# Attention scores of two heads in turns in the two row halves of TensorE, and conditioning sums stored chunk by chunk

## The chip, the cores and the metric

The kernel runs on one core of a Trainium2 chip. The metric is the device time of one execution in microseconds. A core has TensorE (PE; its weight loads are listed as PEld), VectorE (DVE), ScalarE (ACT), GpSimd (POOL) and SyncE (SP, which issues nearly all DMA transfers here).

## The reference

One batch of 256 tokens of width 1024 goes through two blocks, all in fp32. Cut to what matters:

```python
# first block
mod = silu(c) @ ada_w + ada_b                 # 6 vectors of 1024
h = rms_norm(x) * (1 + sc1) + sh1
q, kv, gates, u, merge_g = split(h @ w_in)    # 16 heads of 64, 4 key heads
attn = g0 * compressed(q, kv) + g1 * selected(q, kv) + g2 * windowed(q, kv)
x = x + g1 * merge(attn, state_space(u))
x = x + g2 * hier_moe(rms_norm(x) * (1 + sc2) + sh2)     # 32 experts
x = rms_norm(x)
# second block
mod, mod_c = silu(c_2) @ w_mod + b_mod, silu(c_ctx) @ w_mod + b_mod
x = x + gt1 * rmsnorm(neighbourhood_attention(...) , grouped_attention(...))
x = x + gt2 * rmsnorm(moe(...))                          # 32 experts, top 4
```

With 256 tokens every block of 64 keys is selected and the window covers all tokens, so the selected and the windowed branch are both plain causal attention. That is 16 heads x 2 branches = 32 looks of 256 x 256 scores.

## The kernel before, in words

The program is one long list of instructions; in the parts spoken of here PE, ACT, DVE and POOL run exactly in the order in which the program writes them. Weights come through a ring of 2 MB tiles: SP loads the next piece as soon as the oldest one has been released (`used`).

**The stream.** Projections of the first mixer are cut into rows (`block`, `feed`): one credit of `feed(n)` is three PE matmuls (L705, a product of high and low parts), and after certain rows ACT and DVE finish a result. `cut_ahead` splits the next weights (ACT L717, DVE L718).

**The attention of the first mixer.** `Look(n)` is one head of one branch; looks 2k and 2k+1 are a pair whose queries and keys lie in partitions 0 to 63 and 64 to 127. `scores` takes a PSUM tile `sc` (there are two) and multiplies a 64-row slice of the queries with the keys: 128 keys for the first 128 queries (L1282), 256 keys for the others (L1283). Each fp32 matmul is two passes, so a look has four weight loads and four matmuls there. Then `largest` (DVE, L1288 to L1290), `exps` (ACT, L1295, L1296), `scaled` (DVE, L1300 to L1303), `turned` (PE transposes, L1308), `copied` (ACT, L1312), and for a pair `values` (PE, L1326; ACT L1328) and `ended` (DVE, L1333, only for the second branch: every fourth step). The loop over i has 35 steps and is a pipeline: step i does `largest(i)`, `scores(i+1)`, `scaled(i-1)`, `exps(i)`, two credits of the stream, on odd steps the values of pair (i-3, i-2), one turn of the conditioning generator, `turned(i-1)`, and one more credit.

**The conditioning vectors.** A product of a 1024-vector with 1024 x 512 weights is summed on ACT, DVE and POOL into one tile of 128 x 512 partial sums (`sums` L1143, `part` L1958), or by PE into four strips which ACT copies out (`mod_rows`, L460). The sum over the partitions is then made by PE with those partial sums as the stationary operand and a column of ones as the moving one: eight matmuls, two passes each, of 64 columns (`mod_sum` L481, `pick` L469). Vector element 8p+c goes to partition p, so chunk c is every eighth element of the tile.

Of the kernel before, what the change touches and what calls it, by code (L numbers as in the profile page):

```python
# [17 lines left out]
ALU = mybir.AluOpType  # L18
# [3 lines left out]
P = 128  # L22
D = 1024
T = 256
# [133 lines left out]
def _body(tc, nc, a, off, es, stop, dump):  # L158
    V, S, G, PE = nc.vector, nc.scalar, nc.gpsimd, nc.tensor
# [4 lines left out]
    def ps(tag, bufs, name=None):  # L164
        return psum.tile([P, 512], F32, tag=tag, bufs=bufs, name=name or tag)
# [279 lines left out]
    def used(key):  # L445

        released.add(key)
        while ring.used < ring.loaded and ring.pieces[ring.used][0] in released:
            ring.done()

    def mod_rows(key, lhs, into=None):

        w = ring.get(key).rearrange("p (c f) -> p c f", c=8)
        pt = mmps()
        for c in range(8):
            j = c % 4
            PE.matmul(pt[32 * j:32 * j + 32, :], bcast(lhs[:, c, :], [P, 32]), w[:, c, :], start=(c < 4), stop=(c >= 4), tile_position=(0, 32 * j))
        used(key)
        rows = into[:, :512] if into is not None else pp.tile([P, 512], F32, tag="modrows", bufs=2, name="rows")
        S.copy(rows, pt)  # L460
        return rows

    def pick(pt, h, rows, sel=None):

        sel = k("ecol") if sel is None else sel
        n = sel.shape[1]
        rv = rows.rearrange("q (p c) -> q c p", c=8)
        for c in range(8):
            PE.matmul(pt[64 * h:64 * h + 64, n * c:n * c + n], rv[:, c, :], sel, start=True, stop=True, tile_position=(0, 64 * h))  # L469

# [4 lines left out]
    def mod_sum(s, h, dst, bias):  # L475

        r = slice(64 * h, 64 * h + 64)
        pt = trps()
        sv = s.rearrange("q (p c) -> q c p", c=8)
        for c in range(8):  # L480
            PE.matmul(pt[r, c:c + 1], sv[:, c, :], k("ones")[:, 0:1], start=True, stop=True, tile_position=(0, 64 * h))  # L481
        add_bias(dst[r], pt[r], bias[r])
# [182 lines left out]
    pt = trps()  # L665
# [85 lines left out]
    def feed(n):  # L751

        feed.credit += n
        while feed.credit > 0 and (stream or after):
            cost = 1
            if not feed.apart or not cut_up:
                cut_ahead()
            while lows and (len(lows) == len(cut_up) or not feed.apart and lows[0][3] + feed.lag <= feed.done):
                finish_low()
            if stream:  # L760
                _, _, _, products, rows, post = stream[0]
                cost = 4 // rows
                products(feed.row, cut_up[0])
                feed.row += 1
                if feed.row == rows:
                    feed.row = 0
                    stream.popleft(), cut_up.popleft()
                    after.extend([delay, f] for delay, f in post)
            feed.credit -= cost
            for item in after:  # L770
                item[0] -= cost
            for item in [x for x in after if x[0] < 0]:
                after.remove(item)
                item[1]()
            feed.done += cost
            while feed.done > feed.next:
                feed.next += STEP0
                next(feed.behind, None)
        if not stream and not after:
            feed.credit = 0  # L780
# [333 lines left out]
    def vectors_on():  # L1114

        pending = None
        for tag, v, h in vectors:
            key = (tag, v, h)
            while key not in ring.tiles:
                yield  # L1120
            if tag == "wmod":
                if pending:
                    pending()
                    pending = None
                rows = mod_rows(key, cs2, sums)
                yield
                yield
                pt = trps()
                r = slice(64 * h, 64 * h + 64)
                pick(pt, h, rows, k("esel"))  # L1130
                add_bias((sh3, sc3)[v][r], pt[r], bm[r, v])
                yield
                continue
            w = ring.get(key).rearrange("p (c f) -> p c f", c=8)
            for c in range(0, 8, 2):
                S.activation(w[:, c], w[:, c], AF.Identity, scale=cs[:, c])
                if c:
                    G.tensor_tensor(w[:, 0], w[:, 0], w[:, c], op=ALU.add)
                    V.scalar_tensor_tensor(w[:, 1], w[:, c + 1], cs[:, c + 1], w[:, 1], op0=ALU.mult, op1=ALU.add)
                else:  # L1140
                    V.tensor_scalar(w[:, 1], w[:, 1], cs[:, 1], None, op0=ALU.mult)
                if c == 6:
                    G.tensor_tensor(sums, w[:, 0], w[:, 1], op=ALU.add)  # L1143
                    used(key)
                if c == 4 and pending:
                    pending()
                    pending = None
                yield

            def pending(v=v, h=h, key=key):  # L1150
                mod_sum(sums, h, (gc[:, 0], sh2, sc2, gc[:, 1])[v - 2], ab[:, v])
                summed.append(key)
        if pending:
            pending()
# [112 lines left out]
    class Look:  # L1267
# [7 lines left out]
            self.g, self.gp = 2 * gp + s, gp  # L1275
            self.h = 4 * self.g + self.i

        def scores(self):
            self.pt = pt = ps("sc", 2)
            r = slice(64 * self.s, 64 * self.s + 64)  # L1280
            q, kk = qT[r, self.blk], kz[r, self.br, self.gp]
            PE.matmul(pt[:, :P], q[:, :P], kk[:, :P], start=True, stop=True, tile_position=(64 * self.s, 0))  # L1282
            PE.matmul(pt[:, P:P + T], q[:, P:], kk, start=True, stop=True, tile_position=(64 * self.s, 0))  # L1283

        def largest(self):
            self.e = e = pw.tile([P, 512], F32, tag=f"rot{self.n % 3}", name="e")[:, :384]
# [43 lines left out]
    def ended(pair):  # L1330
        if pair[0].br:
            blk = pair[0].blk
            V.tensor_tensor(ap_[1][:, blk, :], Look.po[:, :T], ap_[0][:, blk, :].bitcast(F32), op=ALU.subtract)  # L1333

    looks = [Look(n) for n in range(32)]
    for n in range(2):
        compressed_scores(n)
        feed(LOOK[0])
    looks[0].scores()
    feed.apart = True  # L1340
    for i in range(35):
        st = looks[i] if i < 32 else None
        prev = looks[i - 1] if 0 < i < 33 else None
        pair = looks[i - 3:i - 1] if i % 2 and i > 2 else None
        if st:
            st.largest()
        if i < 31:
            looks[i + 1].scores()
        if prev:
            prev.scaled()  # L1350
        if st:
            st.exps()
        if lows and len(cut_up) - len(lows) < 2:
            finish_low()
        feed(LOOK[1])
        if pair:
            values(pair)
            ended(pair)
        cut_ahead()
        next(feed.behind, None)  # L1360
        if i < 2:
            compressed_weights(i)
        if i == 4:
            compressed_turned(0)
            compressed_turned(1)
        if prev:
            prev.turned()
            prev.copied()
        feed(LOOK[2])
# [565 lines left out]
    def conditions():  # L1935

        ready, fresh = None, 0
        for i in range(9):
            if i < 8:
                key = ("wmod", 2 + i // 2, i % 2)  # L1940
                while key not in ring.tiles:
                    fresh = WAIT2
                    yield
                for _ in range(fresh):
                    yield
                fresh = 0
                w = ring.get(key).rearrange("p (c f) -> p c f", c=8)
                s = pk.tile([P, 512], F32, tag="part", bufs=2, name="part")
            for c in range(0, 8, 2):
                if i < 8:  # L1950
                    S.activation(w[:, c], w[:, c], AF.Identity, scale=cs2[:, c, 0:1])
                    if c:
                        G.tensor_tensor(w[:, 0], w[:, 0], w[:, c], op=ALU.add)
                        V.scalar_tensor_tensor(w[:, 1], w[:, c + 1], cs2[:, c + 1, 0:1], w[:, 1], op0=ALU.mult, op1=ALU.add)
                    else:
                        V.tensor_scalar(w[:, 1], w[:, 1], cs2[:, 1, 0:1], None, op0=ALU.mult)
                    if c == 6:
                        G.tensor_tensor(s, w[:, 0], w[:, 1], op=ALU.add)  # L1958
                        used(key)
                if c == 4 and i:  # L1960
                    v, h = 2 + (i - 1) // 2, (i - 1) % 2
                    mod_sum(ready, h, (gc[:, 2], sh4, sc4, gc[:, 3])[v - 2], bm[:, v])
                    summed.append(i)
                    if i == 8:
                        return
                yield
            ready = s
# [884 lines left out]
```

## Time and profile before

| | |
|---|---|
| median of the runs, lowest to highest | 2046.55 us, 2046.46 to 2049.3 us (3 runs) |
| the profiled execution | 2040.22 us, span of its instructions 2038.5 us |
| busy in the span | PE 1767.2 us (87%), PEld 990.5 (49%), DVE 854.2 (42%), ACT 544.2 (27%), POOL 258.6 (13%) |
| mean granted TensorE clock | 0.931 of full |
| DMA | 630.82 MB, mean 309 GB/s |

Busy time of PE is modelled from pipelined matmuls, so the distance between starts says more than the busy time. The profile also gives the idle time before an instruction and what ended it; "issue" there means that nothing which the profile shows was waited for.

### The profile page before, as it was taken

What the parts mean: (1) busy time and instruction counts of PE and PEld (TensorE: products, weight loads), DVE (VectorE), ACT (ScalarE), POOL (GpSimd) and SP (SyncE); (2) the same over time, 40 slices, a digit from 0 to 9 for tenths busy, and PEclk for the clock granted to TensorE, in tenths of its full rate; (3) what the DMA queues carried; (4) which work ended last, traced back from release to release, by engine and by line L of the source; (5) the groups of instructions that cost most, each with busy time, mean ns of one, the idle gap of its engine ahead of it and who ended that gap; (6) DMA issues with size and microseconds to landing.
All of it is one profiled execution on the core that took longest, in us unless ns stands there. A gap on an engine that the chain in (4) does not pass through costs nothing. (4 is left out here: it accounts for less than half of the span.)

```text
span 2038.5 us, 25531 instructions
## 1 busy us (share of the span) xinstructions
PE 1767.2 (87%) x10043; PEld 990.5 (49%) x10043; DVE 854.2 (42%) x1832; ACT 544.2 (27%) x1184; POOL 258.6 (13%) x232
## 2 busy tenths in 40 slices
PE   5898999998898997899999689886899889999865
PEld 3766777876445536678864123332233333333211
DVE  7998878543312237886644112211121221221112
ACT  4442566332001115565532011110021111121001
POOL 2576312110000003630110000000000000000000
PEclk8898889898999998899979899998899999999986
DMA  8634235867889977743347999999999999899996
GB/s 262 232 114 161 99 124 179 276 239 271 319 319 395 393 294 214 256 172 94 151 167 326 420 420 419 425 422 422 416 422 419 421 423 419 340 420 418 424 421 252
DMA packets 172666, 630.82 MB, mean 309 GB/s; under 512 B 25424, under 2 KB 32016, under 8 KB 152048
## 3 DMA queue, kind: packets, MB, share of 16 engines
q1 hardware_dynamic: 172112, 628.04, 79.3%
q8 instruction: 89, 1.46, 0.3%
q10 hardware_dynamic: 288, 0.52, 0.1%
q0 software_dynamic: 128, 0.39, 0.1%
q14 instruction: 49, 0.40, 0.1%
HBM read 627.88 MB, written 1.05 MB: 309 GB/s over the span
## 5 line engine op out<-in xcount | busy, mean ns | idle before, releaser
L2553 PE MATMUL mm<-w,xT 128*64 128x512 f32 x1472 | 329.3, 601 | 1.3 <-DMA w<-in_w_gu 1.3
L2553 PEld LDWEIGHTS mm<-w,xT 128*64 128x64 f32 x1472 | 102.8, 138 | 204.2 <-issue 197.4
L2644 PE MATMUL o<-w,aT 128*64 128x512 f32 x640 | 150.7, 606 | 2.5 <-DMA w<-in_w_dn 2.5
L2587 PE MATMUL mm<-w,xT 128*32 128x512 f32 x768 | 104.6, 675 | 39.9 <-DMA w<-in_w_gu 39.9
L2562 DVE TENSOR_SCALAR g<-mm 128x512 f32<-128x512 f32 x23 | 15.9, 692 | 262.7 <-PE mm L2553 262.7
L2821 POOL TENSOR_TENSOR fin<-acc,fin 128x512 f32<-128x512 f32 x1 | 1.3, 1275 | 975.6 <-DVE acc L2819 975.6
L718 DVE TENSOR_TENSOR lo<-w,hi 128x512 fp32r<-128x512 f32 x126 | 102.2, 824 | 26.9 <-ACT hi L717 24.9
L705 PE MATMUL mm<-hTh,scratch 128*128 128x256 f32 x392 | 98.3, 317 | 10.0 <-DVE scratch L718 10.0
L717 ACT CAST hi<-w 128x512 fp32r<-128x512 f32 x126 | 76.7, 620 | 62.0 <-PE mm L705 54.2
L2619 PE MATMUL o<-w,aT 128*32 128x512 f32 x384 | 69.1, 752 | 25.7 <-DMA w<-in_w_dn 23.9
L2644 PEld LDWEIGHTS o<-w,aT 128*64 128x64 f32 x640 | 45.1, 139 | 87.5 <-issue 80.3
L2564 ACT ACTIVATE s<-g 128x512 f32<-128x512 f32 x23 | 14.5, 632 | 272.9 <-DVE g L2562 272.9
L705 PEld LDWEIGHTS mm<-hTh,scratch 128*128 128x128 f32 x392 | 71.7, 204 | 28.1 <-issue 14.1
L1657 PE MATMUL mm<-w,xT 128*32 128x512 f32 x640 | 74.4, 612 | 6.6 <-DVEq L1843 2.7
L2659 DVE SCALAR_TENSOR_TENSOR yl<-yy,wc,yh 128x512 fp32r<-128x512 f32 (+1 forms) x30 | 21.4, 748 | 137.4 <-ACT yh L2658 137.2
L2587 PEld LDWEIGHTS mm<-w,xT 128*32 128x32 f32 x768 | 23.0, 117 | 108.1 <-DMA w<-in_w_gu 61.9
L705 PE MATMUL mm<-hT3h,lo 128*128 128x256 f32 x192 | 60.6, 316 | 8.7 <-DVE lo L718 6.1
L2649 ACT COPY yy<-o 64x512 f32<-64x512 f32 x40 | 23.2, 580 | 157.6 <-PE o L2644 157.2
L1632 PEld LDWEIGHTS sc<-Sm,x 128*128 128x128 f32 x256 | 61.6, 334 | 6.6 <-issue 5.0
L2674 DVE TENSOR_TENSOR acc<-acc,sc 128x512 f32<-128x512 f32 x56 | 37.0, 685 | 66.4 <-PE sc L2666 66.4
L1632 PE MATMUL sc<-Sm,x 128*128 128x128 f32 x256 | 63.1, 410 | 1.3 <-DVE Sm L1623 1.2
L705 PE MATMUL mm<-scratch 128*128 128x256 f32 x216 | 63.8, 295 | 0.0
(706 smaller groups left out, 3532.0 us busy)
## 6 DMA issues: line engine op xcount, KB each, us to landing
w<-in_w_gu SPq DMA_DIRECT2D x128, 2048.0 KB, 20.3
w<-in_w_dn SPq DMA_DIRECT2D x63, 2048.0 KB, 23.2
w<-in_w_in SPq DMA_DIRECT2D x20, 2048.0 KB, 9.5
w<-in_moe_w_gate SPq DMA_DIRECT2D x32, 1024.0 KB, 10.5
w<-in_moe_w_up SPq DMA_DIRECT2D x32, 1024.0 KB, 12.5
w<-in_moe_w_down SPq DMA_DIRECT2D x32, 1024.0 KB, 13.8
w<-in_ada_w SPq DMA_DIRECT2D x12, 2048.0 KB, 9.8
w<-in_w_mod SPq DMA_DIRECT2D x12, 2048.0 KB, 8.9
```

The source lines that it names most:

```text
L705: PE.matmul(out, x, y, start=start and i == 0, stop=stop and i == 2)
L717: S.copy(hi, src)
L718: return parts, lambda: V.tensor_tensor(lo, src, hi.bitcast(F32), op=ALU.subtract)
L1632: PE.matmul(pt[:, P * cc:P * cc + P], xv1[:, n, c, :], Sm[:, n].rearrange("p e s -> p (e s)"), start=(n == 0), stop=(n == 1))
L1657: PE.matmul(pg[32 * j:32 * j + 32, :].rearrange("p (j f) -> p j f", j=2), xT[:, c, 32 * j:32 * j + 32], w[:, c % 2], start=(c == 0), stop= ...
L2553: PE.matmul(pg[i][64 * j:64 * j + 64, :], bcast(ident[:, q:q + 1], [P, 64]) if c < 0 else xT[:, c, :], bgu if c < 0 else w[:, o:o + 512], ...
L2587: PE.matmul(pg[32 * t:32 * t + 32, :], xT[:, c, :], w[:, 512 * ij:512 * ij + 512], start=False, stop=(c == 7), tile_position=(0, 32 * t))
L2619: PE.matmul(pd[32 * t:32 * t + 32, :], aT[:, f % 4, 2 * (1 - e) + f // 4, :], w[:, 512 * j:512 * j + 512], start=False, stop=(f == 7), til ...
L2644: PE.matmul(pd[64 * j:64 * j + 64, :], aT[:, f % 4, f // 4, :], w[:, 512 * j:512 * j + 512], start=False, stop=(f == 7), tile_position=(0, ...
L2649: S.copy(y[:, 512 * j:512 * j + 512], pd[64 * j:64 * j + 64, :])
L2659: V.scalar_tensor_tensor(yl[:, o], y[:, o], back[1], yh[:, o].bitcast(F32), op0=ALU.mult, op1=ALU.subtract)
L2674: V.tensor_tensor(o, o, pc, op=ALU.add)
```

## The change

`scores` becomes `score(n)`, one of the two products of a look. `both_scores` issues them for a pair in turns: first product of the head in rows 0 to 63, first product of the head in rows 64 to 127, then the two second products. The first pair is issued ahead of the loop. In the loop `scores(i+1)` is gone from each step; on odd steps `both_scores` of looks i+1 and i+2 stands after the two credits of the stream, ahead of `values`.

The partial sums are stored with chunk c contiguous (64 elements in a row): ACT's copy in `mod_rows` and POOL's last add now write with a step of 64 elements, and the weight loads of `pick` and `mod_sum` read 64 neighbouring elements where they read every eighth.

```diff
+    def by_chunk(t):
+        return t.rearrange("q (c p) -> q p c", c=8)
...
-        S.copy(rows, pt)
+        S.copy(by_chunk(rows), pt.rearrange("q (p c) -> q p c", c=8))
...
-        rv = rows.rearrange("q (p c) -> q c p", c=8)
+        rv = rows.rearrange("q (c p) -> q c p", c=8)
...
-        sv = s.rearrange("q (p c) -> q c p", c=8)
+        sv = s.rearrange("q (c p) -> q c p", c=8)
...
-                    G.tensor_tensor(sums, w[:, 0], w[:, 1], op=ALU.add)
+                    G.tensor_tensor(by_chunk(sums), w[:, 0].rearrange("q (p c) -> q p c", c=8), w[:, 1].rearrange("q (p c) -> q p c", c=8), op=ALU.add)
...
-        def scores(self):
-            self.pt = pt = ps("sc", 2)
+        def score(self, n):
+            if n == 0:
+                self.pt = ps("sc", 2)
             r = slice(64 * self.s, 64 * self.s + 64)
             q, kk = qT[r, self.blk], kz[r, self.br, self.gp]
-            PE.matmul(pt[:, :P], q[:, :P], kk[:, :P], start=True, stop=True, tile_position=(64 * self.s, 0))
-            PE.matmul(pt[:, P:P + T], q[:, P:], kk, start=True, stop=True, tile_position=(64 * self.s, 0))
+            if n:
+                PE.matmul(self.pt[:, P:P + T], q[:, P:], kk, start=True, stop=True, tile_position=(64 * self.s, 0))
+            else:
+                PE.matmul(self.pt[:, :P], q[:, :P], kk[:, :P], start=True, stop=True, tile_position=(64 * self.s, 0))
...
+    def both_scores(pair):
+        for n in range(2):
+            for st in pair:
+                st.score(n)
...
-    looks[0].scores()
+    both_scores(looks[0:2])
...
             st.largest()
-        if i < 31:
-            looks[i + 1].scores()
         if prev:
             prev.scaled()
...
         feed(LOOK[1])
+        if i % 2 and i < 31:
+            both_scores(looks[i + 1:i + 3])
         if pair:
             values(pair)
```

The add into `part` (L1958) changes as the one into `sums` does.

## Rows read from the trace of the kernel before

**Rows 1.** Page, part 2: DMA share of 40 equal slices, in tenths.
```profile
DMA  8634235867889977743347999999999999899996
```

**Rows 2.** Stretches: us, busy (x instructions) PE, PEld, DVE, ACT, POOL; clock; DMA share, GB/s.
```profile
213.00:333.00 120.00, 114.54 (x717) 87.84 (x716) 96.88 (x338) 73.27 (x209) 33.77 (x25) 0.89 0.33 117
370.00:420.00 50.00, 50.00 (x362) 40.51 (x362) 18.44 (x33) 15.10 (x24) 7.37 (x6) 0.88 0.86 269
800.00:920.00 120.00, 106.97 (x706) 87.42 (x706) 101.40 (x217) 69.27 (x161) 53.65 (x49) 0.91 0.65 223
1030.00:2038.00 1008.00, 852.20 (x4154) 311.02 (x4152) 223.58 (x446) 146.96 (x295) 7.08 (x12) 0.93 0.95 393
```

**Rows 3.** Weight loads grouped by line and shape: count, busy us, mean ns; idle before.
```profile
L1632 PEld LDWEIGHTS sc<-Sm,x 128*128 128x128 f32 x256 | 61.6, 334 | 6.6 <-issue 5.0 <-DVE Sm L1623 1.6
...
L481 PEld LDWEIGHTS tr<-C,sums 128*64 128x64 f32 x128 | 16.1, 215 | 0.7
...
L1070 PEld LDWEIGHTS tr<-w,lk 128*64 128x64 f32 x32 | 4.2, 137 | 2.3
```

**Rows 4.** Weight loads in order of time: start us, length us of the whole run.
```profile
207.90 1.87 PEld L1230 LDWEIGHTS sc<-kcz,qT 128*128 128x128 f32 x16
...
217.29 1.99 PEld L481 LDWEIGHTS tr<-C,sums 128*64 128x64 f32 x16
```

**Rows 5.** Matmuls around one look's scores, in order of time.
```profile
261.92 0.28 PE L705 MATMUL mm<-scratch,third 128*128 128x256 f32 x1
262.03 0.28 PE L705 MATMUL mm<-hTh,third 128*128 128x256 f32 x1
262.24 0.49 PE L1282 MATMUL sc<-kz,qT 64*128 64x128 f32 x2
...
263.09 0.39 PE L705 MATMUL mm<-hTh,third 128*128 128x256 f32 x1
```

**Rows 6.** The weight load after those scores, with the idle time before it.
```profile
263.09 0.19 PEld L705 LDWEIGHTS mm<-hTh,third 128*128 128x128 f32 x1 [0.33 <-issue]
```

**Rows 7.** Second mixer: a pair's scores, eight matmuls in the two row halves in turns.
```profile
931.44 0.28 PE L705 MATMUL mm<-hT3h,hi 128*128 128x256 f32 x1
931.65 0.70 PE L2099 MATMUL sc<-kbT,qbT 64*128 64x256 f32 x4
...
932.72 0.39 PE L705 MATMUL mm<-hT3h,lo 128*128 128x256 f32 x1
```

**Rows 8.** Attention loop after a pair of the second branch, in order of time.
```profile
271.05 0.55 PE L1308 MATMUL tr<-C,e 128*128 128x128 f32 x3
...
271.56 0.42 DVE L1333 TENSOR_TENSOR attnT<-o,attnT 128x256 fp32r<-128x256 f32 x1 [2.35 <-ACT attnT L1328]
...
273.24 0.35 DVE L1303 TENSOR_SCALAR e<-e,su 128x256 f32<-128x256 f32 x1
...
273.54 0.55 PE L1308 MATMUL tr<-C,e 128*128 128x128 f32 x3
```

**Rows 9.** Groups of ACT and POOL: count, busy us, mean ns; idle before.
```profile
L460 ACT COPY sums<-mm 128x512 f32<-128x512 f32 x4 | 2.3, 586 | 17.6 <-PE mm L457 17.6
...
L491 ACT COPY g1b<-tr 128x512 f32<-128x512 f32 x2 | 2.2, 1076 | 5.3 <-PE tr L490 5.3
...
L1143 POOL TENSOR_TENSOR sums<-w 128x512 f32<-128x512 f32 x8 | 11.0, 1378 | 1.3 <-DVE w L1139 0.7
...
L1063 POOL TENSOR_TENSOR lk<-kx,posT 128x960 f32<-128x960 f32 x1 | 2.6, 2592 | 0.0
```

**Rows 10.** DVE beside POOL in the loop, in order of time.
```profile
279.61 1.27 POOL L1138 TENSOR_TENSOR w<-w 128x512 f32<-128x512 f32 x1 [26.65 <-ACT w L1136]
279.65 1.26 DVE L1290 TENSOR_SCALAR mx<-mx 128x2 f32<-128x2 f32 x1
```

**Rows 11.** Start of the kernel: the last pick and what waited for it.
```profile
40.88 2.08 PE L469 MATMUL sc<-C,rows 128*64 128x1 f32 x16 [1.82 <-ACT rows L460]
...
43.00 0.17 DVE L473 TENSOR_TENSOR sc<-sc,ab 128x8 f32<-128x8 f32 x1 [0.58 <-PE sc L469]
```

More of the change, by code (lines that the diff above doesn't have):

```diff
@@ L1957, in conditions @@
                     if c == 6:
-                        G.tensor_tensor(s, w[:, 0], w[:, 1], op=ALU.add)
+                        G.tensor_tensor(by_chunk(s), w[:, 0].rearrange("q (p c) -> q p c", c=8), w[:, 1].rearrange("q (p c) -> q p c", c=8), op=ALU.add)
                         used(key)
```

## The prediction

> **What bounds the kernel now.** I read the DMA slices first. The reader is to see that from about the twenty-second slice on (1030 us) DMA is full: the second mixture of experts runs at the pace of its weights [rows 1]. But that stretch can't begin before routing, which comes at the end of everything before it. So time won ahead of 1030 us moves the whole stretch forward, as long as the earlier part isn't limited by DMA itself. The table of stretches comes next: in the attention loop (213 to 333 us) PE is busy 114.5 of 120 us, DVE 96.9, and DMA only a third; from 370 to 420 us PE is busy all the time, with DMA at 0.86; in the second mixer's start (800 to 920 us) PE has 107 and DVE 101 of 120 us [rows 2]. The changed instructions lie in these three stretches and in the first 45 us. In all of them PE leads, in the loop and the second mixer with DVE close behind. That closeness is what the sum has to be cut for.
>
> The sum is made against the profiled execution, 2040.2 us. The median of the runs is 2046.55 us, 0.3% above it; I subtract the gain from the median. A difference below about 0.2%, 4 us, can't be told from none.
>
> **The sums of the conditioning vectors.** One group is 16 weight loads of 64 columns with one or two moving columns each. There are 24 groups: 8 of L481 on `sums` (217 to 378 us), 8 on `part` (810 to 918 us), and 4 + 4 of L469 (24 to 41 and 389 to 417 us). The group in the rows takes 1.99 us for 16 loads: 15 pitches and a last load of 0.215, so 0.118 a load; the next thing on PE starts 2.0 us later, 0.125 a load [rows 3, 4]. What would a contiguous load take? Single loads of 64 columns from neighbouring elements last 137 ns, those of every eighth element 215 [rows 3]. The same step in 128-column loads (L1632) lasts 334 ns, and contiguous ones 0.19 us [rows 3, 6]. The pitch is told by L1230: 16 contiguous loads of 128 columns in 1.87 us, (1.87 - 0.19) / 15 = 0.112 each, so 0.056 for 64 columns if pitch goes with columns [rows 4, 6]. No row has 64 contiguous columns with so few moving ones, so the bounds are 0.056 and, if small matmuls have a floor of their own, the present 0.125. I take 0.056, since the difference of the single durations, 215 - 137 = 78 ns a load, says nearly the same as 0.125 - 0.056 = 69. A group saves 16 x 0.069 = 1.1 us, at most 16 x 0.078 = 1.25.
>
> The Trainium skill speaks against this: "TensorE: Matmul & The Clock Gate", section "LDWEIGHTS (loading the stationary operand)", makes the time of a load a matter of the column count alone, 64 / 1.2 = 53 ns for 64 columns, an estimate by that page. By it storing chunks contiguously would save nothing; the durations of 215 and 137 ns for the same 64 columns go against it.
>
> **Where these savings reach the end.** *Start:* only the last pick is on the path; DVE's next step of the chain waits 0.58 us for it [rows 11]. ACT's copy becomes slower (below), so 0.5 us, between 0 and 1. *Loop:* six groups, 6.6 us if PE leads throughout. Where DVE has the last word a PE saving is lost; DVE fills 97 of 120 us [rows 2], so I take two thirds, 4.5. *345 to 420 us:* two groups and four picks, 6.6 us; PE is busy throughout from 370 on, one of the two groups lies before, and DMA at 0.86 leaves it little room to start its loads earlier [rows 2]. I take 5. *800 to 920 us:* eight groups, 8.8 us, DVE at 101 against PE at 107 [rows 2]: half, 4.5.
>
> **What the new order of storing costs.** ACT's eight copies write with a step of 64 elements. ACT's nearest row is a copy of the same size with a step of eight on the writing side: 1076 against 586 ns [rows 9]. That is 0.5 us for each; behind the copies `pick` follows two turns of the generator later (in the loop's tail), so only the last one at the start shows, counted there. POOL's 16 last adds take 1378 ns. POOL's nearest row with a step is L1063, 2592 ns for 960 elements, 2.7 ns an element, or 1382 for 512 [rows 9]: nothing. That step is on the reading side; if writing costs POOL what it costs ACT, 1076 / 586 = 1.84 times, an add takes 2.5 us. I take nothing, as the row is of the same engine, and keep +1.15 us an add. It could matter because a small DVE operation lasted 1.26 us while a POOL addition of 1.27 us ran [rows 10]: what POOL gains in length, DVE can lose. The next tile's load, which the add releases, would be later by as much; with DMA at a third it is hidden in the loop.
>
> **The scores.** A look costs PE, from the last stream matmul to the next, 263.09 - 262.03 = 1.06 us, where the normal pitch is 0.11: 0.95 us for a look, 1.90 for two. A third of it is the gap of 0.33 us in which PE's loads stand still after the scores [rows 5, 6]. The second mixer already issues a pair in turns: 932.72 - 931.44 = 1.28, less 0.11, 1.17 us for eight matmuls of 256 columns [rows 7]. The new pair has four of 256 and four of 128, so 1.17 is its upper bound; halving two of the four rounds can't take more than 0.3 off. I take 1.1. A pair so saves 0.8 us (0.73 to 1.0), through one gap instead of two and through loads and matmuls of the two halves side by side. 16 pairs: 12.8 us, if PE leads.
>
> It doesn't all the time. Every fourth step DVE waits for the values (2.35 us idle), then does `ended`, `largest` and `scaled`, up to 273.24 + 0.35 = 273.59, and PE's next transposes start at 273.54, just as DVE is done [rows 8]. From the transposes at 271.05 to these PE has had a credit, a look's scores and two credits to do. The change takes the scores (0.95) out of just this stretch and puts them ahead of the values: there PE will arrive 0.8 to 0.9 us early and wait for DVE. That happens once per two pairs, 8 times: 8 x 0.85 = 6.8 us, though the values themselves come 2 x 0.95 - 1.1 = 0.8 us earlier per pair, which is the gain already counted. So 12.8 - 6.8 = 6 us with no help, and up to 12.8 if DVE also finds its inputs sooner. In two pairs PE's own work is 12.1 us before and 10.5 after; DVE's, by its share in the loop, 12.1 x 97 / 120 = 9.8. The cycle can't get shorter than DVE's 9.8, nor does it quite reach 10.5; I take 11.1, 1.0 us a cycle, 8 us in all.
>
> The pair needs both `sc` tiles free: `largest(i)` must be done before the second head's matmuls. It stands first in DVE's step, two credits and one `scaled` ahead, so no wait is counted; queued behind it on PE would be the values, and DVE's `ended` behind these.
>
> **Sum:** 0.5 + 4.5 + 5 + 4.5 + 8 = 22.5 us: 2017.7 for a profiled execution, 2046.55 - 22.5 = 2024 us for the median. Own range 2014 to 2033.
>
> **The rivals.** *All of it counts* (DVE is pulled along): 1 + 6.6 + 6.6 + 8.8 + 12.8 = 36 us, 2010.5 us. For it: PE is busy in every one of these stretches. Against: DVE's share. *Few columns have a floor of their own:* groups stay at 2.0 us whatever the step, only the scores pay: 8 us, 2038.5. For it: no row with 64 contiguous columns and one moving; against: 215 and 137 ns. By the page of the Trainium skill named above, "TensorE: Matmul & The Clock Gate", the groups would stay as long for another reason, with the same time. *DVE takes over at once:* loop and second mixer give nothing but 2 us between them, 0.5 + 5 + 2 = 7.5 us, 2039. For it: the tight hand-over at 273.5 us and the DVE shares; against: DVE still idles 23 us in the loop. *The gain is swallowed by weights that come no earlier:* 2046.5. Against: DMA at a third in the loop. *POOL's strided writes hold DVE* (the other side): 14 of the 16 adds stand beside the loop and the second mixer. Each microsecond that they get longer can cost DVE 14 us there. With 2.5 us an add that is 14 x 1.15 = 16 us, a gain of 6; slower than before by 0.2% it gets when an add passes 1.38 + 26.6 / 14 = 3.3 us, and at 3.6 us the time is 2055. Nothing in the trace shows POOL that slow in such an add.
>
> **How the numbers follow.** Forecast 0.52; all of it 0.14; floor 0.10; DVE at once 0.13; swallowed 0.06; POOL 0.05. The likeliest gives 2024 us. The range goes from 2010 us (all of it) to 2040 us (floor and DVE at once are in), and leaves out the last two and some of the ends of the first ones, under 0.2. Faster by over 0.2% (under 2042.5 us): 0.52 + 0.14 + 0.10 + 0.13 = 0.89; within 0.2%: 0.06; slower: 0.05.
>
> **What would show it.** The groups of L481 and L469: 16 loads in about 1.0 us instead of 2.0, single loads near 137 ns. A pair's four lines of scores: about 1.1 us up to the next work on PE, and the gap of 0.33 us once a pair or not at all. In the loop: PE idle before L1308 after each fourth step, released by DVE L1303, some 0.8 us. The loop ends about 12 us earlier, the second mixture of experts starts some 22 us earlier and takes as long as before. POOL's adds near 1.4 us, ACT's L460 near 1.1. I am wrong if the loads stay at 215 ns, if PE's waits for DVE in the loop exceed 12 us, or if the 1008 us of the last stretch grow.

## The result and the profile after

The change is faster: 2020.68 us (median of 4 runs, 2020.03 to 2024.68) against 2046.51 us (4 runs); the ratio is 0.9877, with a 95% interval from 0.9859 to 0.9894. The forecast was 2024 us. The profiled executions lie 19.35 us apart, 2040.22 and 2020.87 us, since the one profiled before was faster than each of the four runs.

The slices of the page after, DMA share in tenths as in [rows 1], and the same stretches as [rows 2]:

```profile
DMA  8624337976899986742457999999999999899996
```

```profile
213.00:333.00 120.00, 96.46 (x778) 77.33 (x777) 107.37 (x363) 78.21 (x225) 38.58 (x29) 0.94 0.42 132
370.00:420.00 50.00, 44.87 (x353) 36.63 (x353) 23.94 (x42) 20.56 (x33) 13.20 (x13) 1.00 0.87 305
800.00:920.00 120.00, 102.87 (x742) 80.26 (x742) 105.20 (x235) 71.39 (x170) 45.63 (x44) 0.93 0.57 192
1030.00:2019.00 989.00, 841.30 (x4068) 297.17 (x4067) 212.89 (x409) 141.33 (x279) 2.38 (x3) 0.93 0.96 396
```

In the attention loop PE falls from 114.5 to 96.5 us of 120 while DVE rises from 96.9 to 107.4: DVE now has the larger share, in the loop and in the second mixer. Part of DVE's rise is that the same 120 us hold more of the loop (363 DVE instructions against 338). The last stretch is full of DMA as before; it begins 22.0 us earlier (DVE's first `ordr` at 1041.24 us against 1063.28).

The weight loads, against [rows 3] by line and shape (count, busy us, mean ns; idle before), and against [rows 4] in order of time (start, length of the run):

```profile
L1645 PEld LDWEIGHTS sc<-Sm,x 128*128 128x128 f32 x256 | 61.6, 335 | 6.6 <-issue 5.0 <-DVE Sm L1636 1.6
...
L485 PEld LDWEIGHTS tr<-C,sums 128*64 128x64 f32 x128 | 8.9, 146 | 1.0 <-issue 0.3
...
L1074 PEld LDWEIGHTS tr<-w,lk 128*64 128x64 f32 x32 | 4.2, 137 | 2.3
```

```profile
207.43 1.87 PEld L1234 LDWEIGHTS sc<-kcz,qT 128*128 128x128 f32 x16
...
240.56 1.01 PEld L485 LDWEIGHTS tr<-C,sums 128*64 128x64 f32 x16
```

A single load of the sums takes 146 ns where it took 215, and 16 of them 1.01 us where they took 1.99. The loads whose reading was not changed (L1645, L1074, L1234) last what they lasted. The pitch is (1.01 - 0.146) / 15 = 0.058 us; 0.056 was forecast. The Trainium skill ("TensorE: Matmul & The Clock Gate", section "LDWEIGHTS (loading the stationary operand)") makes 64 columns 53 ns, an estimate by that page, by their count alone; the contiguous pitch of 0.058 us nearly agrees, the 0.118 us worked out from [rows 4] for every eighth element does not.

The storing side, against [rows 9] (same columns):

```profile
L464 ACT COPY sums<-mm 128x512 f32<-128x512 f32 x4 | 4.3, 1076 | 11.4 <-PE mm L461 11.4
```

```profile
L1971 POOL TENSOR_TENSOR part<-w 128x512 f32<-128x512 f32 x8 | 11.4, 1419 | 5.1 <-DVE w L1967 4.1 <-DVE su L2140 0.7
L1147 POOL TENSOR_TENSOR sums<-w 128x512 f32<-128x512 f32 x8 | 10.9, 1360 | 2.3 <-DVE w L1143 1.8
```

ACT pays 0.49 us a copy for the step of 64, as its row of another copy had told. POOL pays nothing: 1360 ns against 1378 for `sums`, 1419 against 1409 for `part`.

A pair's scores, against [rows 5], as matmuls in order of time:

```profile
258.61 0.28 PE L709 MATMUL mm<-hTh,third 128*128 128x256 f32 x1
258.82 0.49 PE L1291 MATMUL sc<-kz,qT 64*128 64x128 f32 x4
259.14 0.60 PE L1289 MATMUL sc<-kz,qT 64*128 64x256 f32 x4
259.67 0.87 PE L1334 MATMUL o<-eT,vt 128*64 128x256 f32 x8
```

From the last stream matmul to the next work on PE it is 1.06 us, less the pitch of 0.11: 0.95 us for a pair. That is what one look took before. Why shows in PE's first matmuls of the scores, up to 262.4 us before and up to 258.95 us after:

```profile
262.24 0.37 PE L1282 MATMUL sc<-kz,qT 64*128 64x128 f32 x1
```

```profile
258.82 0.38 PE L1291 MATMUL sc<-kz,qT 64*128 64x128 f32 x2
```

One matmul of a single look lasts 0.37 us, and two of a pair, one of each head, are over within 0.38 us: they start 7 ns apart, and so do the three pairs of matmuls that follow. The two row halves work at the same time.

And the step behind a pair of the second branch, against [rows 8], in order of time on PE and DVE:

```profile
265.49 0.55 PE L1316 MATMUL tr<-C,e 128*128 128x128 f32 x3
...
266.01 0.42 DVE L1341 TENSOR_TENSOR attnT<-o,attnT 128x256 fp32r<-128x256 f32 x1 [1.40 <-ACT attnT L1336]
...
267.49 0.29 DVE L1310 TENSOR_SCALAR e<-e,su 128x128 f32<-128x128 f32 x1
267.69 0.35 DVE L1311 TENSOR_SCALAR e<-e,su 128x256 f32<-128x256 f32 x1
267.92 0.61 PE L1316 MATMUL tr<-C,e 128*128 128x128 f32 x3 [0.82 <-DVE e L1310]
```

PE now stands idle for 0.82 us ahead of these transposes; 0.85 was forecast. In the steps behind the loop's first seven `ended` such a wait lasts 0.81 to 1.60 us, 8.4 us together. Over the whole loop these waits are (waiting line, releaser: us in total, times, longest), before and after:

```profile
PE tr L1308 <- DVE e L1302: 4.2, 6, 1.5
```

```profile
PE tr L1316 <- DVE e L1310: 21.1, 17, 3.4
```

PE is no longer the engine that leads there, so what counts more is what DVE itself waits for. The same for DVE, for the values and for the scores, before and after:

```profile
DVE attnT L1333 <- ACT attnT L1328: 14.6, 7, 4.0
DVE e L1288 <- PE sc L1283: 4.1, 3, 2.2
```

```profile
DVE attnT L1341 <- ACT attnT L1336: 11.4, 7, 3.4
DVE e L1296 <- PE sc L1289: 0.2, 1, 0.2
```

With 1.5 us more for the sums before, that is 20.2 us of waits before and 11.6 after. DVE's work in the loop is 107.5 and 108.3 us. Work and waits together fall short of the loop's length below by 3.7 us both times, and by 3.5 to 3.9 us in all twelve kernels of this study. So the loop lasts as long as DVE works and waits, and a change gains there what it takes off DVE's waits.

Where the time came from is best read between landmarks that every kernel has. The loop runs from ACT's first `pcm` to DVE's last `ended`; the tail from there to DVE's first `lg` of the first routing; the second mixer's sums from ACT's first `zr` to its last `oaTh`; the last stretch from DVE's first `ordr` to its last `acc`.

| us | loop | tail | second mixer's sums | last stretch |
|---|---|---|---|---|
| before | 131.39 | 75.52 | 154.10 | 966.30 |
| the change | 123.59 | 62.72 | 153.00 | 969.00 |
| difference | -7.80 | -12.80 | -1.10 | +2.70 |

The last stretch has nothing of the change in it; over the twelve kernels of this study it took 966.3 to 971.65 us, and the one profiled before was the quickest. A difference of a few us in one stage of one trace is therefore no finding, and stages are compared over several kernels below.

### The profile page after: what moved, and what is told of

Read it like the earlier page. It is cut to its first block, busy times and chain, and to the rows that moved or that the text cites. A ratio compares the mean times of both kernels' runs of the same rounds, so it can differ in the third digit from the quotient of the medians.

```text
span 2019.1 us, 25531 instructions
## 1 busy us (share of the span) xinstructions
PE 1728.3 (86%) x10043; PEld 956.1 (47%) x10043; DVE 859.4 (43%) x1832; ACT 545.9 (27%) x1184; POOL 257.6 (13%) x232
## 5 line engine op out<-in xcount | busy, mean ns | idle before, releaser
L709 PE MATMUL mm<-hTh,scratch 128*128 128x256 f32 x392 | 93.4, 315 | 9.6 <-DVE scratch L722 9.6
L2632 PE MATMUL o<-w,aT 128*32 128x512 f32 x384 | 70.9, 780 | 23.0 <-DMA w<-in_w_dn 21.1
L1645 PEld LDWEIGHTS sc<-Sm,x 128*128 128x128 f32 x256 | 61.6, 335 | 6.6 <-issue 5.0
L1645 PE MATMUL sc<-Sm,x 128*128 128x128 f32 x256 | 63.2, 409 | 1.3 <-DVE Sm L1636 1.2
```

The source lines that it names most:

```text
L709: PE.matmul(out, x, y, start=start and i == 0, stop=stop and i == 2)
L1645: PE.matmul(pt[:, P * cc:P * cc + P], xv1[:, n, c, :], Sm[:, n].rearrange("p e s -> p (e s)"), start=(n == 0), stop=(n == 1))
L2632: PE.matmul(pd[32 * t:32 * t + 32, :], aT[:, f % 4, 2 * (1 - e) + f // 4, :], w[:, 512 * j:512 * j + 512], start=False, stop=(f == 7), til ...
```

## The experiments

The experiments were run in three batches. The kernels of a batch share 12 or 13 runs of the kernel before, whose median was 2044.4, 2043.82 and 2045.44 us. The difference that counts is that of the ratios.

**The sums alone.** The kernel before with the `by_chunk` lines of the diff alone; the scores stay one look a step.

```diff
+        S.copy(by_chunk(rows), pt.rearrange("q (p c) -> q p c", c=8))
...
+        rv = rows.rearrange("q (c p) -> q c p", c=8)
...
+        sv = s.rearrange("q (c p) -> q c p", c=8)
...
```

> The contiguous sums alone, scores one look at a time as before. Theory A (the groups pay where PE leads, the rest of the gain is the scores'): groups near 1.09 us, some 15 us less than before (loop 5, tail after the loop 10, second mixer 1, start 1 us later), and the stretches of half clock that follow the groups in the kernel before get fewer. Rival B (the gain comes from the scores, the groups are covered by DVE): under 8 us less than before.

Measured: 2029.99 us, ratio 0.9922 (0.9897 to 0.9948). Between landmarks: loop 129.06, tail 64.89, second mixer's sums 152.72. The sums are worth most of the change, as theory A has it, but in the loop only 2.3 us instead of 5: PE's waits for DVE ahead of the transposes rise from 4.2 to 10.6 us there.

**The scores alone.** The changed kernel with the sums stored and read as before.

```diff
-        S.copy(by_chunk(rows), pt.rearrange("q (p c) -> q p c", c=8))
+        S.copy(rows, pt)
...
-        sv = s.rearrange("q (c p) -> q c p", c=8)
+        sv = s.rearrange("q (p c) -> q c p", c=8)
...
```

> The paired scores alone, partial sums stored as before. Theory A: the loop 6 to 10 us shorter, nothing else moves, so 6 to 10 us less than before; the stretches of half clock behind the groups stay. Rival B: the tail after the loop gains too (weights come earlier), 15 us or more less than before.

Measured: 2036.19 us, ratio 0.9950 (0.9937 to 0.9962), theory A. Loop 122.88, tail 74.15, sums 157.23. The loop's 8.5 us are DVE's waits, which fall by 4.2 us for the values and by 3.9 for the scores:

```profile
DVE attnT L1337 <- ACT attnT L1332: 10.4, 7, 3.3
DVE e L1292 <- PE sc L1285: 0.2, 1, 0.2
```

The loop is as short as with the whole change (123.59), so with the new scores in place the six shorter groups there give nothing. PE's wait shows where they went:

```profile
PE tr L1312 <- DVE e L1306: 15.6, 15, 3.4
```

With short groups it is 21.1 us: 5.5 us more, for six groups of 1.0 us saved. DVE's waits hardly change, 11.4 us in all here and 11.6 with the change.

**A pair without turns.** All four products of a pair are issued in one place still, but one head after the other.

```diff
-        for n in range(2):
-            for st in pair:
+        for st in pair:
+            for n in range(2):
                 st.score(n)
```

> The whole change, but a pair's four products one head after the other instead of in turns. Theory A (the two row halves work side by side): a pair takes 0.85 us in turns and 2 x 0.85 - 0.33 = 1.37 us here, 16 x 0.5 = 8 us more PE work in the loop; since DVE has the last word in about half of it, 2 to 6 us slower than the whole change. Rival B (the saving is only the one gap of 0.33 us instead of two): a pair takes 0.85 us here too, same time.

Measured: 2020.84 us, ratio 0.9881 (0.9856 to 0.9906), the same as the change. In its trace, matmuls in order of time:

```profile
260.94 0.50 PE L1291 MATMUL sc<-kz,qT 64*128 64x128 f32 x4
261.27 0.61 PE L1289 MATMUL sc<-kz,qT 64*128 64x256 f32 x4
261.81 0.76 PE L1334 MATMUL o<-eT,vt 128*64 128x256 f32 x6
```

The pair takes 261.81 - 260.94 = 0.87 us, against 0.85 in turns. The saving comes from issuing two looks in one place; the turns add nothing. But the rows show more than either theory has. The program writes both products of the first head ahead of those of the second, and all four matmuls of the first products (L1291, both heads) still start ahead of those of the second ones (L1289). Up to 261.1 us there are two of them again, 14 ns apart:

```profile
260.94 0.39 PE L1291 MATMUL sc<-kz,qT 64*128 64x128 f32 x2
```

So the two halves work side by side in either order, and the description of the kernel ahead, by which PE runs exactly in the program's order, does not hold here: these matmuls did not start in the order in which the program writes them. One gap less would have given rival B only 2 x 0.85 - 0.33 = 1.37 us; its 0.85 came for theory A's reason. By the Trainium skill ("TensorE: Matmul & The Clock Gate", section "The mechanism") PE pulls the load for another row group ahead of matmuls in flight; if so, the order inside a pair need not matter, and the two traces agree with that.

**The values first.** The pair's scores behind `values` and `ended`.

```diff
-        if i % 2 and i < 31:
-            both_scores(looks[i + 1:i + 3])
         if pair:
             values(pair)
             ended(pair)
+        if i % 2 and i < 31:
+            both_scores(looks[i + 1:i + 3])
```

> The whole change with the pair's scores issued after the values instead of ahead of them. Theory A (PE's wait of 0.8 us for DVE after every second pair comes from the scores standing ahead of the values): that wait goes, and after the other pairs DVE waits longer for its scores; the loop 2 to 5 us shorter than with the whole change. Rival B (DVE's work sets the loop, it is busy 89% there): within 1.5 us of the whole change, or slower.

Measured: 2016.42 us, ratio 0.9864 (0.9837 to 0.9890). The loop takes 118.37 us, 5.2 less than with the change, theory A's 2 to 5 us and a little more. That is clear of the spread between traces: the six kernels with pairs of scores ahead of the values have loops of 122.79 to 123.59 us. Tail and sums are within the spread of the others. PE's waits for DVE fall:

```profile
PE tr L1316 <- DVE e L1310: 16.3, 14, 3.5
```

In the steps behind the first seven `ended` they are 4.2 us now, where they were 8.4. The 0.8 us that the change put between the transposes and the values was thus paid for in the loop: DVE's waits for the values fall from 11.4 to 4.5 us, while those for the scores rise from 0.2 to 2.2 (the rows stand with the experiment on the scores behind the transposes). The granted clock of the loop is 0.96 here and 0.93 with the change; what share of the gain that is, the runs don't show.

**The values first only where a pair ends.**

```diff
+        ends = bool(pair and pair[0].br)
-        if i % 2 and i < 31:
+        if i % 2 and i < 31 and not ends:
             both_scores(looks[i + 1:i + 3])
         if pair:
             values(pair)
             ended(pair)
+        if i % 2 and i < 31 and ends:
+            both_scores(looks[i + 1:i + 3])
```

> The pair's scores stand behind the values only in the steps in which a pair ends (every fourth step), ahead of them in the others; all else is the changed kernel. Theory A (what costs is that the scores are taken out of the stretch between the end of a pair and its successor's transposes): as good as moving them in every step, 2014.5 to 2018.5 us, PE's waits for DVE ahead of the transposes under 16 us in the loop. Rival B (the order counts in every step): 2018 to 2021 us.

Measured: 2019.10 us (2018.34 to 2021.87), ratio 0.9883 (0.9864 to 0.9902), loop 120.64 us with 18.2 us of those waits: rival B's time, and a loop halfway. Three of the 5.2 us come back. Of the 2.3 us that are missing nearly all stand in a single place, between the loop's first two `ended`: 236.50 to 253.58 us, 17.08 us, against 14.93 with the values first everywhere. From there on the distances differ by 0.23 us at most, so that the order counts in every step, as rival B has it, is not shown. By time alone it can't be told from the change, nor well from the kernel with the values first everywhere (2014.95 to 2019.78).

**The scores behind the transposes.** One place further back.

```diff
-        if i % 2 and i < 31:
-            both_scores(looks[i + 1:i + 3])
         cut_ahead()
...
             prev.copied()
+        if i % 2 and i < 31:
+            both_scores(looks[i + 1:i + 3])
         feed(LOOK[2])
```

> The pair's scores one place further back, behind the transposes of the step. Theory A (each step later leaves DVE its inputs sooner, as long as the largest of the next look need not wait): the time stays within 3 us of 2016.4 us, the loop at 116 to 120 us. Rival B (DVE's next step begins with the largest of a look whose scores now come last, so DVE waits for them on every odd step, 0.5 us or more 16 times): the loop takes 124 us or more, the time 2021 us or more, with DVE's waits ahead of the largest above 8 us.

Measured: 2023.64 us, ratio 0.9902 (0.9883 to 0.9921), loop 123.67 us. The loop is 5.3 us longer than with the values first, nearly rival B's; its named wait, DVE's `largest` for the scores, is there, with 5.7 us instead of over 8. It makes 3.5 us of the loss, and later values another 1.6. DVE's waits in the loop, first of this kernel and then of the one with the values first:

```profile
DVE attnT L1341 <- ACT attnT L1336: 6.1, 7, 2.8
DVE e L1296 <- PE sc L1289: 5.7, 8, 1.5
```

```profile
DVE attnT L1341 <- ACT attnT L1336: 4.5, 6, 1.5
DVE e L1296 <- PE sc L1289: 2.2, 3, 1.0
```

Of the three places tried the middle one is the best: ahead of the values the scores delay the end of a pair, behind the transposes they are late for the next look.

**The values first, with the old sums.**

```diff
-        sv = s.rearrange("q (c p) -> q c p", c=8)
+        sv = s.rearrange("q (p c) -> q c p", c=8)
```

(and the other `by_chunk` lines likewise)

> The pairs' scores behind the values, and the conditioning sums stored as before the change (groups of 2.0 us). Theory A (in the loop DVE sets the pace, so the longer groups there are hidden whatever the order): the loop, from the start of its first step to its last end, takes 117 to 120 us, as with short groups (118.4), and the time is 13 to 15 us above the kernel with short groups, 2029 to 2032 us, all of it behind the loop. Rival B (with the values first PE leads the loop again, and the six groups there count): the loop takes 122 to 125 us and the time is 2033 to 2038 us.

Measured: 2033.50 us, ratio 0.9943 (0.9924 to 0.9962). The loop takes 118.65 us with long groups against 118.37 with short ones. That settles it for the loop: once the scores are issued in pairs, PE's groups are hidden under DVE in either order. The time is 1.5 us above theory A's range and so just inside rival B's, but rival B's loop of 122 to 125 us did not come: what the short groups save, they save behind the loop.

**Every one-column matmul twice.** The changed kernel; a group has 32 contiguous loads and takes 2.0 us again.

```diff
-            PE.matmul(pt[r, c:c + 1], sv[:, c, :], k("ones")[:, 0:1], ...)
+            for _ in range(2):
+                PE.matmul(pt[r, c:c + 1], sv[:, c, :], k("ones")[:, 0:1], ...)
```

(`pick` likewise)

> Every one-column matmul of the conditioning sums is issued twice, with contiguous loads, so each of the 24 groups has 32 loads and lasts about 2.0 us again; all else is the changed kernel. Theory A (the length of a run of one-column matmuls brings the half-clock stretches behind the groups): the stretches between 205 and 423 us come back, 17 to 23 us lost there instead of 10, and the time is that of the kernel with only the scores changed, 2032 to 2038 us. Rival B (the stretches belonged to loads that read every eighth element, or to chance): the loss stays near 10 us, and only PE's work comes back where PE leads: 2024 to 2030 us.

Measured: 2035.75 us, ratio 0.9962 (0.9948 to 0.9975): the gain of the sums is gone (the scores alone have 0.9950), so it lay in the groups' length on PE, and nowhere else in the storing. The time is theory A's, its clock is not: from 205 to 423 us some 0.06 x 218 = 13 us were lost, by the estimate below, where theory A gave 17 to 23 us and rival B near 10. Loop 122.79, tail 71.86, sums 155.79. What the tail is made of stands in its row; the columns are those of [rows 2]. In turn before, scores alone, groups twice, values first with old sums (all with groups of 2.0 us), and the change:

```profile
343.91:419.43 75.52, 70.33 (x516) 59.89 (x516) 36.55 (x60) 28.03 (x47) 10.34 (x8) 0.91 0.87 286
```

```profile
336.63:410.78 74.15, 70.87 (x517) 61.08 (x517) 35.54 (x60) 27.97 (x47) 10.34 (x8) 0.88 0.89 294
```

```profile
339.02:410.88 71.86, 66.92 (x612) 57.63 (x612) 35.96 (x61) 29.61 (x47) 10.36 (x8) 0.95 0.90 303
```

```profile
332.88:403.54 70.66, 65.45 (x517) 57.72 (x517) 36.53 (x61) 27.89 (x47) 10.35 (x8) 0.98 0.90 301
```

```profile
335.63:398.35 62.72, 59.27 (x517) 51.62 (x517) 37.01 (x61) 29.52 (x47) 9.62 (x7) 0.97 0.94 318
```

One minus the granted clock, times the length, is an estimate of what was lost at 1.2 GHz: 0.09 x 75.52 = 6.8 us before, then 8.9, 3.6 and 1.4, and 1.9 us with the change. Without it the four with long groups take 65 to 69 us, mean 67.9, the change 61, and all eight with short groups 61 to 64, mean 61.9. The six groups of the tail so account for some 6 us, as they should at 1.0 us each; the clock for the rest. On the clock the two theories stay open: the long groups brought back part of the loss here, but hardly any in the kernel with the values first.

**The start as before.** The `rows` copies are stored and read as before, all else is the change.

```diff
-        S.copy(by_chunk(rows), pt.rearrange("q (p c) -> q p c", c=8))
+        if into is None:
+            S.copy(rows, pt)
+        else:
+            S.copy(by_chunk(rows), pt.rearrange("q (p c) -> q p c", c=8))
...
+        rv = rows.rearrange("q (p c) -> q c p" if sel is None else "q (c p) -> q c p", c=8)
...
-        rv = rows.rearrange("q (c p) -> q c p", c=8)
```

> The conditioning rows at the start are stored as before the change (quick copies on ACT, loads of every eighth element), all else is the changed kernel. Theory A (the start became later because ACT's slower copies lie on its chain): DVE's step behind the last pick comes at 42.8 to 43.3 us instead of 44.17, and the time is about 1 us shorter, 2018.5 to 2020.5 us. Rival B (the 1.17 us were a difference in the arrival of weights): it stays at 43.8 us or later, and the time at 2020 to 2022 us.

Measured: 2021.17 us, ratio 0.9899 (0.9882 to 0.9915). DVE's step behind the last pick came at 45.09 us, not earlier: rival B. The chain's own rows, ACT, PE and DVE in order of time, of the change and of this kernel; [rows 11] is the same place before:

```profile
41.94 1.05 ACT L464 COPY rows<-mm 128x512 f32<-128x512 f32 x1 [0.21 <-PE mm L461]
43.04 1.09 PE L473 MATMUL sc<-C,rows 128*64 128x1 f32 x16 [1.24 <-ACT rows L464]
44.17 0.17 DVE L477 TENSOR_TENSOR sc<-sc,ab 128x8 f32<-128x8 f32 x1 [0.39 <-PE sc L473]
```

```profile
42.35 0.56 ACT L465 COPY rows<-mm 128x512 f32<-128x512 f32 x1
42.97 2.08 PE L476 MATMUL sc<-C,rows 128*64 128x1 f32 x16 [0.79 <-ACT rows L465]
45.09 0.17 DVE L480 TENSOR_TENSOR sc<-sc,ab 128x8 f32<-128x8 f32 x1 [0.58 <-PE sc L476]
```

From the copy's start to DVE it takes 44.17 - 41.94 = 2.23 us with the change and 45.09 - 42.35 = 2.74 without: 0.51 us saved, although the copy itself is 0.49 us longer. The chain merely began later in the change's profiled execution. Over the twelve traces DVE's step came between 42.7 and 47.0 us.

**The second mixer's sums as before.** The eight `part` groups are read every eighth element again, all else is the change.

```diff
-                        G.tensor_tensor(by_chunk(s), w[:, 0].rearrange("q (p c) -> q p c", c=8), w[:, 1].rearrange("q (p c) -> q p c", c=8), op=ALU.add)
+                        G.tensor_tensor(s, w[:, 0], w[:, 1], op=ALU.add)
...
-                    mod_sum(ready, h, (gc[:, 2], sh4, sc4, gc[:, 3])[v - 2], bm[:, v])
+                    mod_sum(ready, h, (gc[:, 2], sh4, sc4, gc[:, 3])[v - 2], bm[:, v], "q (p c) -> q c p")
```

> The eight sums of the second mixer are stored as before the change, so their groups take 2.0 us again; all else is the changed kernel. Theory A (DVE sets the second mixer's pace): the eighth sum's end comes at most 2 us later against the routing ahead of it, and the time rises by 0 to 2 us, 2020 to 2023 us. Rival B (PE leads there, as the prediction had half): 5 to 8 us more, 2025.5 to 2029 us.

Measured: 2026.49 us (2022.26 to 2031.30), ratio 0.9917 (0.9901 to 0.9933). The time is in rival B's range, but its stage is not: in the trace the second mixer's sums take 155.82 us against 153.00, 2.8 us more. Another 3.5 us had been lost by 212 us, where the kernels do not differ, and 2.6 us in the last stretch. One trace is too little, so all twelve: the five with long `part` groups take 154.1 to 158.7 us, mean 156.3; the seven with short ones 151.3 to 155.0, mean 153.0. The groups are worth 3.3 us there, between the two theories. Their rows, before and with the change, columns as in [rows 2]:

```profile
769.08:923.18 154.10, 130.99 (x863) 109.90 (x864) 128.66 (x251) 87.02 (x196) 68.10 (x56) 0.88 0.65 209
```

```profile
748.18:901.18 153.00, 125.47 (x863) 103.89 (x864) 131.94 (x251) 86.85 (x196) 67.66 (x56) 0.88 0.64 209
```

PE has 5.5 us less to do, and the stage is 1.1 us shorter: DVE, with 132 of 153 us, has the larger share there. Its work and its waits make up the stage to within 3.0 to 3.4 us in all twelve kernels. With long groups DVE works 129.0 us and waits 24.1 on average, with short ones 132.7 and 17.2: it saves 6.9 us of waiting and loses 3.7 again, since the same instructions take longer. Why they do is not shown; the storing it is not, since the kernel with groups twice stores as the change does and has 129.6 us.

## Why the prediction was right, point by point

The time came out 3.3 us below the forecast, well inside the range. The terms were less even than the sum, and that the sum came out so well is in part luck: 4.5 us too much in the loop and 4.3 too little in the tail cancel.

| term, us | forecast | measured | read from |
|---|---|---|---|
| start | 0.5 | 0.5 | the chain behind the last copy |
| scores in pairs | 8 | 8.5 | loop, scores alone against before |
| six groups in the loop | 4.5 | 0 | loop, the change against scores alone |
| 345 to 420 us | 5 | 9.3 | tail, four kernels with long groups (mean 73.05) against eight with short ones (63.79) |
| second mixer's sums | 4.5 | 3.3 | five kernels against seven |
| sum | 22.5 | 21.6 | |

The medians differ by 25.8 us, and the interval of the ratio makes that 22 to 29; the sum of the stages is just short of it, and the 4 us that remain lie within what the last stretch and the start vary by; where they come from is not shown.

**The loads.** Right. 1.0 us a group was saved, 1.1 forecast. The rival in which few columns have a floor of their own is out.

**The storing.** Right on both engines: 0.49 us on ACT, nothing on POOL. The rival of POOL's strided writes is out; the bound of 2.5 us an add, carried over from ACT's ratio, was wrong for POOL.

**The scores.** Right in size and reason. A pair saves 0.95 us, 0.8 forecast, and the two halves do work side by side, since their matmuls start 7 ns apart. The change takes turns for it, which isn't needed: issuing both looks in one place does it. A cycle of two pairs, from one `ended` to the next around 265 us, takes 10.70 and 10.94 us where it took 12.13; 11.1 was forecast. PE's wait behind the end of a pair was 0.81 to 1.60 us, 8.4 in all, for 6.8 forecast; the other 12.7 of its 21.1 us were not foreseen. What made the loop shorter is DVE, which "finds its inputs sooner": 8.1 of the 8.5 us are its waits for the values and the scores.

**The groups in the loop.** This step failed. Two thirds of them were counted on top of the scores, with DVE at 97 of 120 us as the only discount. The two savings draw on the same reserve, the 20.2 us that DVE waits before: with the scores alone it is 11.4 us, with the short groups as well 11.6, so the groups took nothing more off it. PE's waits for DVE grew to 21.1 us instead, above the 12 us that the prediction named as the sign of being wrong. Alone the sums give 2.3 us there; behind the scores, nothing. The prediction applied the limit within each term, not to their sum.

**The tail.** Mis-sized, to the other side: 5 forecast, 9.3 measured. All six groups and picks count in full, about 6 us; DMA's 0.86 was not the limit it was taken for (it went to 0.94 in the tail with the change). The rest, some 3 us, is the difference in stretches at half clock, which the prediction did not price; that the change brought it is not shown.

**The second mixer.** Half was taken for DVE, 4.5 of 8.8; 3.3 came. DVE does set the pace there, and its 3.7 us of longer work took part of what it waited less.

**The last stretch.** It grew by 2.7 us, another sign of being wrong by the prediction; that is within the 5.4 us by which it varies between kernels that are alike there.

What the experiments add is the better order: with the values first the kernel takes 2016.42 us, ratio 0.9864 against the change's 0.9877. The intervals overlap, but the loop's 5.2 us and the waits that vanished are shown in the trace. It has the lowest median of the versions run.

## What to carry to other kernels

Operands that are loaded as weights are worth storing contiguously even where another engine pays for it, if that engine is off the path: 0.5 us on ACT bought 1.0 us on PE. When several edits shorten the same engine in one stretch, cut their sum, not each of them, by the slack of the engine next in line, and read the gain from what that engine waits for. And where work is moved in a pipeline written out by hand, try the place on both sides: one place further back here was worth 5 us of the loop, two places cost them again.

## What the runs showed of the hardware

Matmuls in the two row halves of TensorE run at the same time, whichever head the program issues first: eight take 0.85 us in turns and 0.87 us one head after the other, and four of a single head 263.09 - 262.24 = 0.85 us.

Some stretches at half clock stood behind groups of one-column matmuls. The windows of the kernel before, around the group at 365.16 us (columns as in [rows 2]):

```profile
364.00:368.00 4.00, 3.39 (x25) 3.24 (x26) 3.57 (x5) 0.89 (x2) 1.26 (x1) 0.99 1.04 385
368.00:372.00 4.00, 4.00 (x24) 4.00 (x23) 2.07 (x4) 1.16 (x3) 0.00 (x0) 0.59 0.14 49
372.00:376.00 4.00, 4.00 (x36) 3.87 (x34) 2.89 (x3) 2.26 (x5) 2.91 (x2) 1.00 0.42 110
```

A granted clock of 0.59 is most of the stretch at 1.2 GHz, although PE is busy throughout. From 205 to 423 us the granted clock was 0.90 before, 0.91 with the scores alone, 0.94 with groups twice, and 0.95 with the change; but 0.96 in the kernel with the values first and the old sums. In the eight kernels with short groups it was 0.94 to 0.97. So two of the four kernels with long groups lost clearly more and two did not; the long groups may bring the stretches, but not behind each of them, and what decides stays open.

The mean clock over the whole span hardly moved, 0.931 before and 0.930 after: the loop went from 0.90 to 0.93 and the tail from 0.91 to 0.97, but the start up to the loop, which the change hardly touches, from 0.90 to 0.88, and the stages behind the tail stayed as they were to 0.01.
